# Layer 1 of a two-layer decoder step: the memory queries are projected first, and memory attention of the first half is issued beside the window-query projections

## The chip, the cores and the metric

The kernel runs on one core of one Trainium2 chip. The metric is device time in microseconds (us) of that core. Nothing is shared with other cores. Engines are named as in the profile: PE (TensorE matmul), PEld (TensorE weight load), DVE (VectorE), ACT (ScalarE), POOL (GpSimd), SP (SyncE, which issues nearly all transfers).

## The reference, cut to what matters

Two layers (A: gated linear attention, B: sliding-window attention with sinks) run over 512 prompt tokens and 32 sampled tokens (8 sequences of 4), with model width 1024. Everything is float32. Each layer is a half-weighted SwiGLU block, a mixing block, and a second half-weighted SwiGLU block. The change lies in the mixing block of the second layer (layer 1, B):

```
h = rmsnorm(x, mix_norm[1])
qs, mq = split(h @ b_w_in, [768])          # 12 window heads, 4 memory heads, 64 wide
qs = rope_partial(qs)                      # rotary on 16 of 64 lanes
tok = swa(qs, k_shared, v_shared, sinks)   # window of 128, causal, with a sink per head
mo  = softmax(mq @ mem_k.T / 8) @ mem_v    # 256 memory rows per sequence
x = x + concat([tok, mo]) @ b_w_out
x = x + swiglu_half(x, ffn2)
```

For the prompt the memory keys and values are computed from `mem_prompt`; for the samples they come from `cache_mem_k` and `cache_mem_v`, one set per sequence.

## The kernel before, in words

Tokens are split into two halves: half 0 holds 256 prompt tokens and the 32 sampled ones (288 columns), half 1 the other 256 prompt tokens. Activations lie with the model dimension on the partitions. A weight block (128 x 1024) is loaded by SP, cut by `halved` into a high and a low part (ACT at L298, DVE at L299), and `dense` (L356) multiplies it in three passes per block of 128 rows. One **unit** is one such block: 24 matmuls for one half.

The two halves are run against each other, so that attention of one half goes beside dense work of the other. In `layer`, for layer 1:

- half 1 still has a chunk of its first SwiGLU block to do, the generator `late`: 16 gate and up units and 8 down units (d0 to d7). Seven of them are issued, then half 0's norm, then half 0's whole projection `project(0, ...)` (`in_b`): six window-query units bq0 to bq5, each followed by the rotary step on DVE (`rope`), then two memory-query units bmq0 and bmq1.
- `attend(0, ...)` (`attend_b`) is woven by `weave` with 18 units of `fill`. `fill` is the rest of `late` (17 units), then half 1's norm `enter(1, ...)` and half 1's projection. Two more units (`pad`) follow, so that three units of half 1's projection come before half 0's output projection `out_proj`; the last five come after it.
- `out_proj` for half 0 needs all of half 0's attention.
- The same is then done with half 1's attention against the first chunk of half 0's second SwiGLU block.

`attend_b` itself weaves two streams. One is `swa_prompt`: six groups, three for each 128-token block. A group is scores (L1134), mask and softmax on DVE and ACT (L1155 to L1170), transposes (L1172), masked copies (L1176) and the product with the values (L1142). It uses banks 3 to 5 of the matmul memory, so one group follows another. The other stream is the chain `mem_prompt` (two blocks of scores L649, softmax L654 to L662, transposes L668, values L679), then, in half 0 only, `swa_sample` (L1188 to L1257), then `mem_sample`. `mem_sample` builds masked queries `qb` (L697), multiplies them with the eight cached key tiles `mkc` (loads L703, matmuls L705), does one softmax and two transposes (L720), and multiplies with eight cached value tiles `mvc` (L726, L733). The memory stream uses banks 6 and 7.

The order of instructions on each engine is fixed when the program is built, by a list scheduler that simulates the program. `high_priority(offset=...)` moves work ahead in it: weight cutting and the emptying of dense results by 6000 (`AHEAD`), the norm steps by 6500 (`SOON`), attention issued through `weave` by 3000 (`LEAD`).

Scratch tiles are 97 numbered slots. `self.u` takes the slot at the front of one queue, `drop` puts slots back at its end, and a `Ring` takes several and gives them back when it is closed. Which slot a tile gets depends only on the order in which the code takes and gives back; the first write to a slot waits for the last reader of what lay in it before. The sum of squares for a norm (`stats`) takes a new slot for its first and its eighth tile (L376) and adds the six between into the first (L381). `rstd` sums the two over the partitions with matmuls against ones (L404), goes on with L410 to L430 on DVE and ACT, spreads the result with L416, and `normed` applies it (L438).

Of the kernel before, what the change touches and what calls it, by code (L numbers as in the profile page):

```python
# [163 lines left out]
def chain(*gens):  # L164
    for g in gens:
        yield from g


def take(gen, n):
    for _ in range(n):  # L170
        if next(gen, StopIteration) is StopIteration:
            return
        yield


def drain(*gens):
    for g in gens:
        for _ in g:
            pass
# [42 lines left out]
def chain_weave(*streams):  # L222
    live = [[g, n, 0] for g, n in streams]
    while live:
        s = min(live, key=lambda e: (e[2] + 1) / e[1])
        s[2] += 1
        if next(s[0], StopIteration) is StopIteration:
            live.remove(s)
        else:
            yield  # L230


class Build:
    NU, NV, NLD, NML = 97, 13, 8, 3
    WB = (3, 4, 4, 2)
    MIX = 10
    FIRST, AHEAD, SOON, LEAD = 20000, 6000, 6500, 3000
    FILL = ((6, 1, 7, 2, 6), (7, 2, 5, 0, 9))
    HOMES = ((13, 8, 3), (8, 8, 3))
# [854 lines left out]
    def in_b(self, h, xs, s):  # L1094
        d = self.d
        n = NH[h]
        s.q, s.mq = [], []
        self.rope_tables(h)
        for j in range(6):
            ps, = self.dense(d["b_q"][j], [xs], f"bq{j}")  # L1100
            s.q.append(self.u(n))
            self.rope(ps, s.q[j], h)
            yield
        for j in range(2):
            ps, = self.dense(d["b_mq"][j], [xs], f"bmq{j}")
            s.mq.append(self.copy(self.u(n), ps))
            if j == 1:
                self.drop(xs, self.tabs[h])
            yield

# [156 lines left out]
    def layer(self, l, project, attend, w_out, xs):  # L1267

        s = [Share(), Share()]
        f1, f2 = f"ffn1_{l}", f"ffn2_{l}"  # L1270
        mix, out = {}, {}

        def enter(h, norm):
            with self.tc.high_priority(offset=self.SOON):
                r = self.rstd(h)
                out = self.normed(h, norm, r)
            self.drop(r)
            return out

        def enter_pair(norm, xs):  # L1280
            with self.tc.high_priority(offset=self.SOON):
                r = self.rstd(1)
                xs[1], xs["forms"] = self.pair(norm, r, xs[0])
            self.drop(r)

        def both(tag, xs):
            drain(self.ffn_pair(tag, 1, xs), self.ffn_pair(tag, 2, xs, gathered=(0,)))
            self.drop(xs[0], self.extra)

        lead, pad, hold, last, more = self.FILL[l]  # L1290
        both(f1, xs)
        late = self.ffn(f1, 0, (1,), xs, gathered=(1,), tanh=True)
        mix[0] = enter(0, f"mix_{l}")
        drain(take(late, lead))
        drain(project(0, mix[0], s[0]))

        def second():
            yield from late
            self.drop(xs[1])
            mix[1] = enter(1, f"mix_{l}")  # L1300
            yield from project(1, mix[1], s[1])

        fill, units = second(), EARLY - lead + (22 if l == 0 else 8) - hold - pad
        self.weave(attend(0, s[0]), (take(fill, units), units))
        drain(take(fill, pad))
        self.drop(s[0].q if l else [])
        drain(self.out_proj(w_out, s[0].toks + s[0].mo, 0))
        out[0] = enter(0, f"ffn2_{l}")
        drain(fill)
        if l == 0:  # L1310
            drain(self.late_mem())
        early = self.ffn(f2, 0, (0,), out, tanh=True)
        more += last
        self.weave(attend(1, s[1]), (take(early, EARLY - more), EARLY - more))
        drain(take(early, last))
        self.drop(s[1].q if l else [])
        drain(self.out_proj(w_out, s[1].toks + s[1].mo, 1))
        enter_pair(f"ffn2_{l}", out)
        drain(early)
        both(f2, out)  # L1320

        def final():
            yield from self.ffn(f2, 0, (1,), out, gathered=(1,), tanh=True)
            self.drop(out[1])
        return final()
# [14 lines left out]
    def attend_a(self, h, s):  # L1340
# [2 lines left out]
        return chain_weave((self.attn_a(h, s), 70 if h == 0 else 54), (chain(self.mem_prompt(0, s.mq, s.mo), *extra), 6 + 9 * (h == 0))), \  # L1343
            (76 if h == 0 else 60)

    def attend_b(self, h, s):
        s.mo = self.parts(2, h)
        s.toks = self.parts(6, h)
        extra = [self.swa_sample(s.q, s.toks), self.mem_sample(1, s.mq, s.mo)] if h == 0 else []
        return chain_weave((self.swa_prompt(h, s.q, s.toks), 13),  # L1350
                           (chain(self.mem_prompt(1, s.mq, s.mo), *extra), 6 + 17 * (h == 0))), (37 if h == 0 else 20)

    def run(self):
        nc, d = self.nc, self.d
# [67 lines left out]
        xk = self.normed(1, "kv", r)  # L1422
        drain(take(first, self.MIX))
        drain(self.shared_kv(1, xk))
# [81 lines left out]
```

## Time and profile before

| what | value |
|---|---|
| median of 3 runs | 2154.74 us (2149.47 to 2155.02) |
| profiled execution, own time | 2148.32 us |
| span in the profile | 2146.5 us |
| PE busy, DVE busy, ACT busy | 96%, 72%, 50% of the span |
| mean granted TensorE clock | 0.983 |

The span runs from the first to the last instruction; 1.8 us of the execution's own time lie around it. In the profile L356 is line 356 of the program, `bank<-u,bq0h` is an instruction that writes a bank of the matmul memory from a scratch slot and the high part of weight block bq0, and text in square brackets is idle time of the engine just before the instruction, with what ended it.

### The profile page before, as it was taken

The numbers are of one execution on the slowest core, as the hardware profiler recorded it, in microseconds if no ns is written. First come the engines' busy times: TensorE is split into PE (matmuls) and PEld (weight loads), VectorE is DVE, ScalarE is ACT, GpSimd is POOL, SyncE is SP. The second block draws the span as 40 slices with busy tenths as digits, with TensorE's granted clock in tenths as the row PEclk, the third lists the DMA queues.
The fourth block names the chain that finished last, engine by engine and source line by source line (L and its number), as shares of the span: only waits on it lengthen the run. The fifth ranks groups of instructions, "written<-read, shape, count | busy, mean of one in ns | idle before, by whom it ended". The sixth has DMA issues, their size and how long they took to land.

```text
span 2146.5 us, 41032 instructions
## 1 busy us (share of the span) xinstructions
PE 2065.4 (96%) x16428; PEld 2000.7 (93%) x16428; DVE 1539.5 (72%) x3234; ACT 1067.2 (50%) x2089; POOL 35.8 (2%) x69
## 2 busy tenths in 40 slices
PE   6999999999999998999999999999998999999998
PEld 6999999998799998999999999999986988999998
DVE  7876675576668869757587776665877877966655
ACT  5554444754646645535355553444544544544434
POOL 5000000000000000000000000000000000000000
PEclk9999999999999999999999999999998999999999
DMA  7533253434454342323354523243443434232344
GB/s 230 157 115 109 79 156 118 138 120 148 152 160 159 125 143 79 108 87 103 113 178 142 177 89 114 74 148 122 151 147 105 143 109 128 89 109 79 110 149 128
DMA packets 90496, 273.03 MB, mean 127 GB/s; under 512 B 11408, under 2 KB 25248, under 8 KB 90272
## 3 DMA queue, kind: packets, MB, share of 16 engines
q1 hardware_dynamic: 89728, 269.87, 39.8%
q8 instruction: 129, 2.11, 0.4%
q14 instruction: 63, 0.52, 0.1%
q10 hardware_dynamic: 576, 0.52, 0.1%
HBM read 264.04 MB, written 7.70 MB: 127 GB/s over the span
## 4 chain that ended last, share of the span: by engine, by line
PE 85%; DVE 8%; DMA 4%; ACT 2%; issue 2%; SPq 0%; DVEq 0%; ACTq 0%
PE bank L356 55%; PE bank L342 21%; PE bank L904 1%; PE bank L1142 1%; DVE u L299 1%; PE bank L1134 1%; DMA u19r<-gu_ffn 0%; PE bank L649 0%; DMA u21r<-gu_ffn 0%; DMA u20r<-gu_ffn 0%; PE bank L705 0%; PE bank L416 0%; PE bank L679 0%; PE bank L1030 0%; PE bank L668 0%
## 5 line engine op out<-in xcount | busy, mean ns | idle before, releaser
L298 ACT ACTIVATE u<-u 128x272 fp32r<-128x272 f32 (+3 forms) x328 | 134.0, 422 | 132.5 <-DVE u L537 55.2
L545 DVE SCALAR_TENSOR_TENSOR x<-bank,x 128x16 f32<-128x16 f32 (+2 forms) x192 | 59.7, 342 | 115.0 <-PE bank L356 114.2
L299 DVE TENSOR_TENSOR u<-u,u 128x272 fp32r<-128x272 f32 (+3 forms) x328 | 137.2, 429 | 3.0 <-ACT u L298 1.2
L356 PE MATMUL bank<-u,d0h 128*128 128x272 f32 (+2 forms) x352 | 71.3, 289 | 0.0
L356 PE MATMUL bank<-u,d1h 128*128 128x272 f32 (+2 forms) x352 | 70.3, 288 | 0.0
L356 PE MATMUL bank<-u,d2h 128*128 128x272 f32 (+2 forms) x352 | 68.6, 289 | 0.4 <-DVE x L755 0.4
L356 PE MATMUL bank<-u,d3h 128*128 128x272 f32 (+2 forms) x352 | 68.0, 290 | 0.0
L356 PE MATMUL bank<-u,d4h 128*128 128x272 f32 (+2 forms) x352 | 67.5, 289 | 0.0
L356 PE MATMUL bank<-u,d5h 128*128 128x272 f32 (+2 forms) x352 | 67.3, 289 | 0.0
L356 PE MATMUL bank<-u,d6h 128*128 128x272 f32 (+2 forms) x352 | 67.1, 288 | 0.0
L356 PE MATMUL bank<-u,d7h 128*128 128x272 f32 (+2 forms) x352 | 67.0, 288 | 0.0
L534 ACT ACTIVATE u<-u 128x272 f32<-128x272 f32 x56 | 24.1, 430 | 73.2 <-DVE u L533 73.2
L356 PEld LDWEIGHTS bank<-u,d0h 128*128 128x128 f32 x352 | 56.3, 188 | 0.2
L356 PEld LDWEIGHTS bank<-u,d2h 128*128 128x128 f32 x352 | 55.4, 188 | 0.9 <-issue 0.5
L356 PEld LDWEIGHTS bank<-u,d1h 128*128 128x128 f32 x352 | 56.1, 188 | 0.0
L356 PEld LDWEIGHTS bank<-u,d3h 128*128 128x128 f32 x352 | 55.3, 188 | 0.3 <-DVE x L580 0.3
L356 PEld LDWEIGHTS bank<-u,d4h 128*128 128x128 f32 x352 | 55.4, 188 | 0.0
L356 PEld LDWEIGHTS bank<-u,d5h 128*128 128x128 f32 x352 | 55.2, 188 | 0.1
L356 PEld LDWEIGHTS bank<-u,d6h 128*128 128x128 f32 x352 | 55.2, 188 | 0.0
L356 PEld LDWEIGHTS bank<-u,d7h 128*128 128x128 f32 x352 | 55.1, 188 | 0.1
L356 PE MATMUL bank<-u,d2l 128*128 128x272 f32 (+2 forms) x176 | 51.0, 290 | 0.0
L356 PE MATMUL bank<-u,d4l 128*128 128x272 f32 (+2 forms) x176 | 50.9, 289 | 0.0
(1178 smaller groups left out, 7664.7 us busy)
## 6 DMA issues: line engine op xcount, KB each, us to landing
g0r<-gu_ffn SPq DMA_DIRECT2D x8, 512.0 KB, 3.5
u0r<-gu_ffn SPq DMA_DIRECT2D x8, 512.0 KB, 3.4
g1r<-gu_ffn SPq DMA_DIRECT2D x8, 512.0 KB, 3.4
u1r<-gu_ffn SPq DMA_DIRECT2D x8, 512.0 KB, 3.5
g2r<-gu_ffn SPq DMA_DIRECT2D x8, 512.0 KB, 3.4
u2r<-gu_ffn SPq DMA_DIRECT2D x8, 512.0 KB, 3.9
g3r<-gu_ffn SPq DMA_DIRECT2D x8, 512.0 KB, 3.5
u3r<-gu_ffn SPq DMA_DIRECT2D x8, 512.0 KB, 3.6
```

What stands on the lines that cost most here:

```text
L298: nc.scalar.activation(h, src, AF.Copy)
L299: nc.vector.tensor_tensor(out=l, in0=src, in1=h.bitcast(F32), op=ALU.subtract)
L342: self.nc.tensor.matmul(ps, a[:, k, :], x, start=start and k == 0 and j == 0, stop=k == len(xs) - 1 and j == 2, skip_group_check=True)
L356: self.nc.tensor.matmul(ps, w[:, k, :], x, start=i == 0 and j == 0, stop=i == kc - 1 and j == 2)
L534: nc.scalar.activation(c2, c2, AF.Silu)
L545: nc.vector.scalar_tensor_tensor(out=x, in0=p, scalar=0.5, in1=x, op0=ALU.mult, op1=ALU.add)
L904: nc.tensor.matmul(pv[:, c * half:(c + 1) * half], lhs[:, c * P:(c + 1) * P], second(rhs[:, c * P:(c + 1) * P]), start=True, stop=True)
L1134: nc.tensor.matmul(ps[:, e, P * (1 - back):][:, :P], q[j][64 * half:64 * half + 64, cols], self.keys(kv, half, n - back), start=True, stop ...
L1142: nc.tensor.matmul(dst, self.vt[n - i][:, 64 * kv:64 * kv + 64], pt[i].rearrange("p g t -> p (g t)"), start=i == 0, stop=i == last)
```

## The change

In `in_b` the two memory-query units come first and the six window-query units after them; the rotary tables are loaded after the memory queries, and the normalised input and the tables are given back after bq5. This holds for both halves. For half 0 of layer 1, once bmq0 and bmq1 are issued, a new function `mem_b` builds the chain `mem_prompt` then `mem_sample`, and its first 9 steps (all 6 of `mem_prompt` and the first 3 of `mem_sample`, which end with the matmuls L705) are woven with the six window-query units. `attend_b` for half 0 goes on with the rest of that chain, 6 steps, and then `swa_sample`, 9 steps, woven with `swa_prompt`; it counts 28 steps where it counted 37, against the same 18 units of `fill`. Half 1 keeps its attention as it was.

```diff
@@ class Build
-    MIX = 10
+    MIX, MEM = 10, 9
@@ in_b
         s.q, s.mq = [], []
+        for j in range(2):
+            ps, = self.dense(d["b_mq"][j], [xs], f"bmq{j}")
+            s.mq.append(self.copy(self.u(n), ps))
+            yield
         self.rope_tables(h)
         for j in range(6):
             ps, = self.dense(d["b_q"][j], [xs], f"bq{j}")
             s.q.append(self.u(n))
             self.rope(ps, s.q[j], h)
-            yield
-        for j in range(2):
-            ps, = self.dense(d["b_mq"][j], [xs], f"bmq{j}")
-            s.mq.append(self.copy(self.u(n), ps))
-            if j == 1:
+            if j == 5:
                 self.drop(xs, self.tabs[h])
             yield
@@ layer
-        drain(project(0, mix[0], s[0]))
+        first = project(0, mix[0], s[0])
+        if l == 1:
+            drain(take(first, 2))
+            self.weave(self.mem_b(s[0]), (first, 6))
+        drain(first)
@@ new, and attend_b
+    def mem_b(self, s):
+        s.mo = self.parts(2, 0)
+        s.mem = chain(self.mem_prompt(1, s.mq, s.mo), self.mem_sample(1, s.mq, s.mo))
+        return take(s.mem, self.MEM), self.MEM
+
     def attend_b(self, h, s):
+        s.toks = self.parts(6, h)
+        if h == 0:
+            return chain_weave((self.swa_prompt(h, s.q, s.toks), 13),
+                               (chain(s.mem, self.swa_sample(s.q, s.toks)), 24 - self.MEM)), 37 - self.MEM
         s.mo = self.parts(2, h)
-        s.toks = self.parts(6, h)
-        extra = [self.swa_sample(s.q, s.toks), self.mem_sample(1, s.mq, s.mo)] if h == 0 else []
-        return chain_weave((self.swa_prompt(h, s.q, s.toks), 13),
-                           (chain(self.mem_prompt(1, s.mq, s.mo), *extra), 6 + 17 * (h == 0))), (37 if h == 0 else 20)
+        return chain_weave((self.swa_prompt(h, s.q, s.toks), 13), (self.mem_prompt(1, s.mq, s.mo), 6)), 20
```

## Rows read from the trace of the kernel before

**Rows 1.** The page: busy time of the engines, and the clock in 40 slices.

```profile
PE 2065.4 (96%) x16428; PEld 2000.7 (93%) x16428; DVE 1539.5 (72%) x3234; ACT 1067.2 (50%) x2089; POOL 35.8 (2%) x69
...
PEclk9999999999999999999999999999998999999999
```

**Rows 2.** Windows: stretch, length, busy time by engine, granted clock, DMA share, GB/s.

```profile
1497.80:1526.90 29.10, 29.10 (x226) 28.82 (x225) 22.18 (x46) 11.34 (x18) 0.16 (x1) 1.00 0.45 147
1526.90:1596.00 69.10, 69.10 (x592) 64.01 (x590) 57.85 (x172) 40.08 (x115) 1.42 (x6) 1.00 0.50 155
1596.00:1637.50 41.50, 30.44 (x315) 20.10 (x314) 22.87 (x98) 12.12 (x50) 0.00 (x0) 0.71 0.33 100
...
1757.00:1776.00 19.00, 15.07 (x113) 11.79 (x114) 13.25 (x59) 5.69 (x27) 0.00 (x0) 0.91 0.09 28
```

**Rows 3.** Waits of PE from 1596 to 1638 us: total, times, longest.

```profile
PE bank L1172 <- DVE u L1170: 5.4, 4, 2.4
```

**Rows 4.** Timeline of PE from 1590 us to half 0's output projection.

```profile
1595.83 0.29 PE L356 MATMUL bank<-u,d7l 128*128 128x256 f32 x1
...
1609.21 1.98 PE L705 MATMUL bank<-mkc,u 128*64 128x256 f32 x8 [1.17 <-DMA mkc<-mk]
1610.97 1.92 PE L1142 MATMUL bank<-u,vt 128*64 128x256 f32 x8
...
1613.93 0.83 PE L404 MATMUL bank<-ones,u 128*128 128x1 f32 x6
...
1621.74 1.98 PE L1142 MATMUL bank<-u,vt 128*64 128x256 f32 x8
...
1627.98 0.43 PE L733 MATMUL bank<-mvc,u 128*32 128x64 f32 x16 [2.37 <-DVE we L1160]
...
1635.83 1.77 PE L1142 MATMUL bank<-u,vt 128*64 128x256 f32 x8
...
1637.58 0.36 PE L356 MATMUL bank<-u,bq0h 128*128 128x256 f32 x1
...
1646.82 0.53 PE L356 MATMUL bank<-u,op0h 128*128 128x288 f32 x2 [0.38 <-DVE u L1047]
```

**Rows 5.** Timelines of ACT and DVE in the same stretch.

```profile
1610.42 0.42 ACT L376 ACTIVATE u<-x 128x256 f32<-128x256 f32 x1 [6.24 <-PE bank L705]
...
1596.16 0.42 DVE L580 SCALAR_TENSOR_TENSOR x<-bank,x 128x256 f32<-128x256 f32 x1 [0.26 <-PE bank L356]
...
1630.13 0.15 DVE L410 TENSOR_SCALAR r<-bank 128x2 f32<-128x2 f32 x1
```

**Rows 6.** Tile bmq1h: duration min/median/max in ns, first and last start.

```profile
L356 PE MATMUL bank<-u,bmq1h x32: 274/290/364, 1523.7 to 1687.9; 128*128 128x288 f32 x16, 128*128 128x256 f32 x16
```

**Rows 7.** Single lines, 1497 to 1640 us (L1142: 1545 to 1600).

```profile
L679 PE MATMUL bank<-u,u x32: 272/273/324, 1544.1 to 1563.8; 128*64 128x128 f32 x32
...
L705 PE MATMUL bank<-mkc,u x32: 379/631/689, 1604.6 to 1616.2; 128*64 128x256 f32 x32
...
L1142 PE MATMUL bank<-u,vt x12: 379/404/430, 1549.9 to 1592.8; 128*64 128x256 f32 x12
...
L1203 PE MATMUL bank<-sck,u x48: 270/272/373, 1564.0 to 1581.4; 64*128 64x128 f32 x32, 128*128 128x128 f32 x16
...
L1257 PE MATMUL bank<-stc,scv x32: 202/254/275, 1599.2 to 1602.6; 128*64 128x8 f32 x32
```

**Rows 8.** Groups by line, DVE, 1526.9 to 1596: busy us, mean ns, idle before.

```profile
L654 DVE TENSOR_REDUCE mx<-bank 128x2 f32<-128x512 f32 x4 | 2.7, 686 | 0.7 <-PE bank L649 0.7
...
L662 DVE TENSOR_SCALAR u<-u,sm 128x256 f32<-128x256 f32 x8 | 2.4, 347 | 0.0
...
L697 DVE TENSOR_TENSOR u<-c_bm,u 64x128 f32<-64x128 f32 x8 | 2.3, 284 | 0.1
```

**Rows 9.** Half 1: first scores (timeline), and line L1142 from 1640 to 1780 us.

```profile
1656.26 1.16 PE L1134 MATMUL bank<-u,u 64*128 64x128 f32 x16
...
L1142 PE MATMUL bank<-u,vt x48: 379/379/657, 1692.8 to 1775.0; 128*64 128x256 f32 x48
```

## The prediction

> **What bounds the kernel now.** Read the page first: PE is busy 96% of the span and granted full clock nearly throughout, with one dent in the clock line about three quarters of the way [rows 1]. A change that removes no work can gain only where PE waits or runs at the lower of its two levels, so the next view is the windows around the changed code [rows 2]. In the first two stretches, half 0's projection and the rest of `late`, PE is busy for every microsecond at full clock. Then 41.5 us follow in which PE is busy for 30.44 at a mean granted clock of 0.71 (2.4 GHz is 1.00, 1.2 GHz is 0.50). That is the tail of half 0's attention, and the only big hole near the change. Three units of half 1's projection come behind it (1637.58 to 1646.82, 9.3 us [rows 4]), and only then half 0's output projection.
>
> Why is the tail bare? The timeline of PE has the last matmul of `late` at 1595.83 and the first of half 1's projection at 1637.58 [rows 4]. Between them PE waits most for softmax steps, 5.4 of its 11.1 idle us [rows 2, 3], with no dense unit to put there, since half 1's projection needs its norm. The timelines of ACT and DVE show why the norm is late [rows 5]: the last update of x is at 1596.16, but its square (L376) stands until 1610.42 behind L705. The count of slots explains that: the eighth square takes the first slot given back by `qb`, and L705 reads `qb`. Then the sums (L404) come at 1613.93 [rows 4], and their reader L410 stands in DVE's order behind attention until 1630.13 [rows 5]. From L410 to the first projection matmul it is 7.5 us. Without the two delays the norm would need from 1596.6 about 0.4 (square), 0.8 (sums) and 7.5 us, so some 10 instead of 42.
>
> **The change, part by part.**
>
> *Memory queries first, both halves.* The same eight units, in another order: bmq0 and bmq1 end about 20 us earlier than before, where the last began at 1523.7 [rows 6] and the projection ended at 1526.9, 3.2 us on. They end at about 1507: from 1497.8 two units of 3.2 and one unit of `late`, 3.1 by the pace of half 1's three units [rows 4]. Each window query comes 6.4 us later. Cost on PE: nothing.
>
> *`mem_prompt` beside the projection.* Its last matmuls started at 1563.8 [rows 7], and all lay inside the stretch where PE is full [rows 2]; they are moved from one full stretch to another, so nothing is won on PE. DVE takes L654, L662 and L697 with it, 7.4 us [rows 8], plus some 1.3 of small steps, into a stretch where it had 29.10 - 22.18 = 6.9 us free [rows 2]. The cutting of weights goes ahead of it, so I cost this at nothing; what hides it is that weights are cut some units ahead. If that cover is gone, PE waits for the overflow, 8.7 - 6.9 = 1.8 us. The bounds are 0 and 2.
>
> *The first three steps of `mem_sample`.* Eight key loads (256 KB each), L697 and the 32 matmuls L705 leave the tail. In the tail L705 took 1.98 us for 8 [rows 4]; at full clock a 256-column matmul in a dense unit takes 0.128 us (9.24 for 72), so 32 cost 4.1 us in the full stretch. Behind them the chain goes on with the value matmuls L733, eight tiles at 0.43 us [rows 4], 3.5 us. `late` then ends up to 7.6 us later than 1596; I take 6, so 1602. The loads join the weight loads in SP's order and wait for three buffers; behind them stand weight loads, and behind those the cutting and the units. The DMA share there is 0.45 to 0.50 against 0.33 in the tail [rows 2]; I cost them at nothing, and 1.2 us (the one wait on such a load [rows 4]) if three weight buffers ahead don't cover.
>
> *Slots.* Counting takes and returns through the new order: the window attention's two rings, 11 slots, now get two slots of a rotary step, the four of `qb`, the two memory queries, two of the last rotary step and one of the normalised input. So the first group of `swa_prompt` can't write its weights before the last L705. By the durations of before, `mem_prompt` takes 1563.8 - 1526.9 = 37 us and L705 12 [rows 7]: 1507 + 37 + 12 = 1556, and about 4 for the rest of the group puts its first value product at 1560. Before it was at 1549.9 [rows 7]. The window chain thus starts about 10 us later. On the other side, the eighth square now gets the slot of `mem_sample`'s probabilities, whose last reader, the transposes L720, is then long past. The 14 us of waiting on L705 go.
>
> *The tail.* The first three value products were about 21 us apart (1549.9 to 1592.5, twelve matmuls in three groups [rows 7]), those in the tail 10.8 apart at best (1610.97 to 1621.74 [rows 4]); the step between 1592.5 and 1610.97 had L705 in front, 6 us with its wait. With the first at 1560 the third falls at 1602, the fourth at 1613, the sixth at 1634.5, and the output projection can start at about 1636. Attention hence ends about where it did (1637.5): what the memory work gives back at the end, the later start takes. The gain is that half 1's norm starts at 1602 and its three units, 9.3 us, run from about 1612 inside the tail and no longer behind it. 1646.8 - 1636.2 = 10.6 us. `swa_sample` comes last now; it took 39 us beside dense work (1564.0 to 1603 [rows 7]) and can start about 20 us after L705 (the rest of `mem_sample` lay between the last L705 at 1616.2 and 1637.5 [rows 4, 7]), at 1576, so it ends by 1615 and does not set the end. Bounds: 1.3 if the three units stay behind, 21 if the window chain is one group ahead.
>
> *A rule beside these rows.* The Trainium skill, page "Perfetto Trace Analysis", section "Identifying the Most-Contended Engine", says that matmul busy time flatters PE and that weight-load busy time should be read. In the tail that is 20.10 of 41.5 us against 30.44 [rows 2]: a hole of 21.4 us by the rule and 11.1 by the row. In the full stretches both are near full, so the rule changes only how much the tail can give.
>
> *Half 1.* Its first window scores started at 1656.26, during half 0's output projection [rows 9]. They need bq0 and bq1; bq1 now comes after that projection. `mem_prompt` can go first in its place. I cost this at nothing, with bounds of 6 us lost (the first group of scores some 20 us later, of which most was waiting: its first value product came only at 1692.8 [rows 9]) and 4 gained (PE idle 3.9 us in the last stretch [rows 2]).
>
> Sum: 2148.3 (the profiled execution) - 10.6 = 2137.7. The median of the runs shown is 6.4 above the profiled execution, so about 2144 as a median.
>
> **The rivals.**
>
> *No change (0.26).* Half 1's norm stays behind attention: L410 stood 15 us in DVE's order after its sums were there [rows 4, 5], with DVE half idle, and a new fixed order can repeat that. The three units then stay behind the tail: gain 1.3, 2153. The Trainium skill, page "TensorE: Matmul & The Clock Gate", the specification table at its head, gives VectorE a strictly ordered queue; by that rule such an instruction can't be overtaken, and the trace agrees with the 15 us.
>
> *More (0.12).* With the memory stream lighter, the window chain is a group ahead when `late` ends. One step of 10.8 us leaves the tail: gain 21, 2133. That uses the whole hole that weight loads show [rows 2]. Against it: the slots make that chain start late.
>
> *Slower (0.18).* The slot wait costs more than I take. The first group waits for L705, and six groups follow in one row. Each us by which its value product comes after 1560 moves the end by one. From 1571 on there is no gain; at 1580, two dense steps late, it is 9 us slower, 2164. For it: `mem_prompt` competes on DVE with six rotary steps, 22.18 of 29.10 us busy already [rows 2]. Against it: without window groups in its way it may run faster than 37 us.
>
> **How the numbers follow.** The forecast has 0.44, the three rivals 0.26, 0.12 and 0.18. The time is that of the forecast, 2144. Its own range is 2136 to 2151. The range for all reaches from 2128 (more than 21 us gained, with half 1's 4) to 2161, which leaves out most of the slower case. A change of 0.3%, 6.5 us, is about what a measurement of this kernel can tell from none: faster (below 2148.3) takes the forecast and the better rival, 0.56; slower (above 2161) 0.17; 0.27 lies between.
>
> **What would show it.** Right: L376 for the eighth square no longer waits on L705; units bmq0, bmq1 and bq0 of half 1 lie among the last window groups, not behind them; the stretch from the end of `late` to half 0's output projection falls from 51 us to about 34, at a granted clock above 0.71; the first L1142 near 1560. Wrong: L410 again far behind L404; PE waits for cut weights between 1498 and 1535; the first L1142 after 1571; half 1's attention ending later against its output projection. Most likely to fail is the date of the first window group, since I took it from durations in another surrounding.

## The result and the profile after

The changed kernel takes 2159.92 us (median of 9 runs, 2155.94 to 2162.02), the kernel before in the same runs 2154.09 (9 runs). The ratio is 1.0031, 95% interval 1.0019 to 1.0042: 5.8 us slower by the medians, where 2144 and a gain was forecast.

One caution ahead of the rows. The two profiled executions differ before the first changed instruction: L410 of half 0's own norm stands at 1477.82 us in the one and at 1483.02 in the other, with the same order of instructions on PE up to there. So what follows is measured from the first matmul of half 0's projection, 1497.8 in the kernel before and 1501.5 in the changed one. From there to the last L510 (the matmuls with which the next SwiGLU block takes over two banks of half 1's attention) it is 277.5 and 285.5 us: 4.3 of the 8 us are lost up to half 0's output projection (149.0 against 153.3), 3.7 behind it (128.5 against 132.2).

The page after the change, to be read against [rows 1]:

```profile
PE 2074.4 (96%) x16428; PEld 2005.3 (93%) x16428; DVE 1541.2 (71%) x3234; ACT 1064.4 (49%) x2089; POOL 34.7 (2%) x69
...
PEclk9999999999999999999999999999997999999999
```

The same number of instructions, but PE is busy 9 us longer. That fits more time at the lower level of the clock: the mean granted clock is 0.980 for 0.983, and the dent has gone from 8 to 7. The windows show the stretches: the projection with the rest of `late`, the tail, and half 1's three units. Columns as in [rows 2].

```profile
1501.40:1605.20 103.80, 103.55 (x949) 95.20 (x949) 82.56 (x221) 52.20 (x134) 0.20 (x1) 1.00 0.57 180
1605.20:1643.90 38.70, 26.84 (x182) 19.20 (x181) 24.82 (x105) 13.88 (x58) 0.10 (x1) 0.65 0.07 22
1643.90:1654.80 10.90, 10.55 (x74) 10.34 (x73) 5.16 (x16) 4.22 (x11) 0.00 (x0) 0.82 0.01 2
```

The full stretch is longer by the memory work that moved into it, as forecast, and PE is idle for only 0.25 us of it. But the tail behind it has lost those matmuls (182 for 315 in [rows 2]) and hardly shrunk, and the three units stand behind it as before, partly at the lower clock (10.9 us at 0.82). The timeline of PE over the tail:

```profile
1605.22 0.36 PE L404 MATMUL bank<-ones,u 128*128 128x1 f32 x2
...
1605.83 0.83 PE L404 MATMUL bank<-ones,u 128*128 128x1 f32 x6
1607.51 0.65 PE L1142 MATMUL bank<-u,vt 128*64 128x256 f32 x4 [0.84 <-DVE u L1176]
...
1612.92 0.43 PE L1172 MATMUL bank<-c_ident,u 128*128 128x128 f32 x2 [3.67 <-DVE u L1170]
...
1615.74 1.98 PE L1142 MATMUL bank<-u,vt 128*64 128x256 f32 x8 [0.52 <-DVE u L1176]
...
1623.87 1.45 PE L1172 MATMUL bank<-c_ident,u 128*128 128x128 f32 x4 [4.14 <-DVE u L1170]
1625.84 1.97 PE L1142 MATMUL bank<-u,vt 128*64 128x256 f32 x8 [0.52 <-DVE u L1176]
...
1642.04 1.95 PE L1142 MATMUL bank<-u,vt 128*64 128x256 f32 x7
...
1654.80 0.53 PE L356 MATMUL bank<-u,op0h 128*128 128x288 f32 x2 [0.35 <-ACT u L362]
```

The value products of four of the six window groups lie behind the end of `late`, where it was three; PE waits for their softmax. Why so late, and why didn't half 1's norm fill the hole? ACT and DVE:

```profile
1605.38 0.40 ACT L376 ACTIVATE u<-x 128x256 f32<-128x256 f32 x1
...
1525.45 0.76 DVE L1155 COPY_PREDICATED bank<-masks,neg 128x256 f32<-128x256 uint8 x2
...
1563.95 0.42 DVE L712 TENSOR_REDUCE smx<-bank 128x1 f32<-128x256 f32 x1
...
1564.68 0.41 DVE L1158 TENSOR_REDUCE wx<-bank 128x2 f32<-128x256 f32 x1
...
1605.43 0.56 DVE L1215 SCALAR_TENSOR_TENSOR u<-bank,u 128x160 f32<-128x160 f32 x2 [0.47 <-PE bank L1208]
...
1622.78 0.75 DVE L1216 TENSOR_REDUCE vx<-u 128x1 f32<-128x160 f32 x3
...
1633.23 0.14 DVE L410 TENSOR_SCALAR r<-bank 128x2 f32<-128x2 f32 x1
```

Four things are to be seen. The eighth square (L376) no longer waits for L705: that step of the forecast holds. The first window group is masked at 1525.45 (L1155), and its maximum (L1158), which needs nothing else, comes 39 us later, directly behind mem_sample's maximum L712. In `swa_sample` the last masked scores are ready at 1605.99 (L1215), and their maxima (L1216) come 16.8 us later, behind the maxima of the fifth window group; its last value product then starts at 1641.9, in the tail, where the forecast had it done by 1615. And the norm's L410 comes 27.4 us after the start of its last sums (16.2 before, [rows 4, 5]). In the kernel before the same pattern was there to be seen and was overlooked: L1155 of the first group at 1513.40, its L1158 at 1534.58, directly behind the two maxima of `mem_prompt`.

```profile
1513.40 0.77 DVE L1155 COPY_PREDICATED bank<-masks,neg 128x256 f32<-128x256 uint8 x2 [0.33 <-PE bank L1134]
...
1533.25 0.69 DVE L654 TENSOR_REDUCE mx<-bank 128x2 f32<-128x512 f32 x1
...
1534.58 0.40 DVE L1158 TENSOR_REDUCE wx<-bank 128x2 f32<-128x256 f32 x1
```

What these steps have in common is where they write: L410, L654, L712, L1158 and L1216 (in `swa_sample`) each open a tile of `self.small` (L281), one ring of 24 buffers under one tag for all streams. The theory tested below is that a ring hands out its buffers in the order in which the code issues their first writes. In the changed kernel `mem_b` issues all tiles of `mem_prompt` ahead of the first window tile, the step behind it issues the one of L712, also ahead, and the norm's tiles come behind those of window groups issued before them. The rivals are the scratch slots, which the prediction counted, DVE's load, and half 1's new order of projections. One more, that 24 buffers are simply too few, is tested by no run, since every edit of the rings also adds buffers; counting the code speaks against it. Between half 0's own norm and the first window maximum only 13 tiles are taken (three by that norm, eight by `mem_prompt`, two by `mem_sample`), so the ring can hardly have run out there.

### The profile page after: what moved, and what is told of

Same layout as the page of the kernel before. It is cut to its first block, busy times and chain, and to the rows that moved or that the text cites. A ratio compares the mean times of both kernels' runs of the same rounds, so it can differ in the third digit from the quotient of the medians.

```text
span 2158.5 us, 41028 instructions
## 1 busy us (share of the span) xinstructions
PE 2074.4 (96%) x16428; PEld 2005.3 (93%) x16428; DVE 1541.2 (71%) x3234; ACT 1064.4 (49%) x2089; POOL 34.7 (2%) x69
## 4 chain that ended last, share of the span: by engine, by line
PE 49%; DVE 7%; DMA 3%; issue 1%; ACT 1%; DVEq 0%; ACTq 0%; SPq 0%
PE bank L356 32%; PE bank L342 13%; PE bank L1142 1%; DMA u20r<-gu_ffn 1%; DMA u18r<-gu_ffn 1%; DMA u19r<-gu_ffn 1%; DMA u21r<-gu_ffn 1%; PE bank L1134 1%; DVE u L299 0%; PE bank L416 0%; PE bank L1172 0%; DVE u L537 0%; PE bank L1203 0%; DVE u L535 0%; PE bank L404 0%
## 5 line engine op out<-in xcount | busy, mean ns | idle before, releaser
L298 ACT ACTIVATE u<-u 128x272 fp32r<-128x272 f32 (+3 forms) x328 | 133.9, 421 | 139.9 <-DVE u L537 61.4
```

The source lines that it names most:

```text
L298: nc.scalar.activation(h, src, AF.Copy)
```

## The experiments

All times are ratios to the kernel before on the same chip, with a 95% interval; from the profile of each run come distances in us. **Group 1** is the first value product L1142, **late** the last d7 matmul and **op** the first matmul of half 0's output projection (in norm_ring the first behind the stall), all from the projection's first matmul; **norm** is from the start of the last row of sums L404 to L410; **half 1** is from op to the last L510; **sum** is op and half 1 together.

| kernel | ratio | group 1 | late | norm | op | half 1 | sum |
|---|---|---|---|---|---|---|---|
| before | 1 | 52.1 | 98.0 | 16.2 | 149.0 | 128.5 | 277.5 |
| the change | 1.0031 (1.0019 to 1.0042) | 76.8 | 102.8 | 27.4 | 153.3 | 132.2 | 285.5 |
| h0_new | 0.9968 (0.9954 to 0.9981) | 45.4 | 113.8 | 11.4 | 145.2 | 128.9 | 274.1 |
| before_h1_new | 1.0018 (1.0007 to 1.0029) | 52.1 | 98.0 | 16.2 | 149.7 | 131.0 | 280.7 |
| order_only | 0.9979 (0.9966 to 0.9993) | 45.4 | 112.5 | 12.5 | 145.2 | 132.8 | 278.1 |
| h1_old | 1.0032 (1.0020 to 1.0043) | 76.8 | 103.8 | 27.4 | 153.4 | 127.6 | 281.0 |
| mem6 | 1.0013 (1.0003 to 1.0022) | 61.4 | 105.2 | 19.9 | 147.8 | 130.7 | 278.5 |
| norm_ring | 1.0033 (1.0020 to 1.0047) | 76.5 | 105.7 | 1.5 | 150.2 | 133.5 | 283.7 |
| window_ring | 1.0033 (1.0020 to 1.0047) | 62.7 | 108.6 | 0.9 | 147.4 | 137.9 | 285.3 |
| two_rings | 1.0031 (1.0017 to 1.0046) | 63.0 | 108.7 | 0.9 | 146.9 | 133.5 | 280.4 |
| mem_rings | 1.0075 (1.0062 to 1.0088) | 70.3 | 106.6 | 24.4 | 153.9 | 136.2 | 290.1 |
| window_prompt_rings | 0.9970 (0.9958 to 0.9982) | 63.9 | 109.6 | 1.4 | 140.4 | 134.6 | 275.0 |
| all_rings | 0.9974 (0.9963 to 0.9985) | 63.1 | 108.4 | 1.4 | 137.8 | 134.3 | 272.2 |
| h1_old_all | 0.9947 (0.9928 to 0.9965) | 63.1 | 108.9 | 1.4 | 141.5 | 124.9 | 266.4 |
| before_norm_ring | 0.9987 (0.9975 to 0.9998) | 51.9 | 97.8 | 0.9 | 141.3 | 133.0 | 274.3 |
| before_all_rings | 0.9927 (0.9915 to 0.9939) | 35.2 | 116.5 | 0.9 | 138.9 | 124.9 | 263.8 |
| before_rings_h1_new | 0.9969 (0.9958 to 0.9981) | 35.2 | 113.6 | 0.9 | 136.3 | 131.9 | 268.3 |
| before_rings_h0_new | 0.9945 (0.9928 to 0.9963) | 45.3 | 120.3 | 2.4 | 142.5 | 122.6 | 265.2 |

Sum and ratio agree to 4 us or better but for order_only (0.6 us longer by its one profile, 4.5 shorter by the ratio); where they differ the ratio, made of many runs, decides. The column op is not the end of half 0's attention in every kernel: in norm_ring, window_ring, two_rings, window_prompt_rings, all_rings, h1_old_all and before_norm_ring the output projection starts ahead of the last group's value product. In these and in before_all_rings it takes 28.9 to 30.9 us from op to the projection's last matmul, in the other ten 26.8 to 27.4; so there 2 to 4 us of what op gains come back in the column half 1.

Since the order of instructions is fixed when the program is built, each edit shifts the whole order, not only the step that it names.

### The rings, on the changed kernel

**norm_ring.** Only the norm's tiles leave the shared ring.

```diff
@@ rstd, L405
-        v, s, t = (self.small("r", 3)[:, :len(blocks)] for _ in range(3))
+        v, s, t = (w[:, :len(blocks)] for w in (lambda w: [w[:, 3 * i:3 * i + 3] for i in range(3)])(self.up.tile([P, 9], F32, tag="smn", name="r", bufs=1)))
```

> The changed kernel, in which only the three small tiles of the normalisation (L405) leave the shared ring of 24 small tiles and have a ring of their own. Theory: the norm's first small step (L410) stands 27 us behind its sums because the shared ring hands its buffers out in the order in which the code issues them, and the last window group's tiles were issued ahead of it. Then L410 follows the sums within about 3 us, half 1's first three units (9.3 us) run ahead of the last two groups of half 0's window attention, and the time falls by about 8 us against the changed kernel, to about 2152 (0.997 to 1.000 of the kernel before). Rival: DVE's load, or the order in which the planner wants the steps, holds L410; then it stays 15 us or more behind the sums and the time stays at 2160 (1.003). Second rival: the units come early but the six window groups are pushed back by as much; then half 1's projection starts at about 1612 and the output projection still at about 1654, and the time is 2158 to 2160.

The mechanism came as expected, the gain did not. L410 follows its sums by 1.5 us and the three units run in the tail, from 1619.42. PE's timeline:

```profile
1612.94 0.83 PE L404 MATMUL bank<-ones,u 128*128 128x1 f32 x6
...
1619.42 0.39 PE L356 MATMUL bank<-u,bmq0h 128*128 128x256 f32 x1 [2.43 <-ACT u L298]
...
1638.49 1.45 PE L1172 MATMUL bank<-c_ident,u 128*128 128x128 f32 x4 [4.96 <-DVE u L1170]
1640.46 1.98 PE L1142 MATMUL bank<-u,vt 128*64 128x256 f32 x8 [0.52 <-DVE u L1176]
...
1655.83 0.85 PE L356 MATMUL bank<-u,op0h 128*128 128x288 f32 x2
```

And two windows, with the units and behind them:

```profile
1612.30:1632.60 20.30, 16.97 (x137) 14.99 (x137) 15.83 (x53) 12.02 (x30) 0.10 (x1) 0.92 0.09 30
1632.60:1660.40 27.80, 21.36 (x135) 15.83 (x134) 17.11 (x70) 9.47 (x41) 0.00 (x0) 0.65 0.21 67
```

Then PE has nothing dense left (it issues six matmuls of op0 and stops) and the last window groups run bare, 27.8 us at a granted clock of 0.65. The hole has moved, not shrunk: the second rival of the expectation.

**window_ring.** Only the window groups' tiles leave, one tile for each pair's maximum, sum and sink; the shared ring shrinks to 18 for room.

```diff
@@ swa_probs, L1156
-        mx, sm, es = self.small("wx", 2), self.small("ws", 2), self.small("we", 2)
+        mx, sm, es = (lambda w: [w[:, 2 * i:2 * i + 2] for i in range(3)])(self.up.tile([P, 6], F32, tag="smw", name="wx", bufs=12))
```

> The changed kernel, in which the three small tiles of each window group (L1156) have a ring of their own (and the shared ring has 18 buffers in place of 24, for room). Theory of the shared ring: the first group's maximum (L1158) waited 39 us behind its mask step (L1155) because its tile comes after those of mem_prompt and mem_sample in the ring. Then L1158 follows L1155 within about 3 us, and the first value product (L1142) comes as soon as L705 has given the slots back, at about 1564 in place of 1578: one group less in the tail, 8 to 12 us under the changed kernel, 2148 to 2152 (0.997 to 0.999). Rival, the scratch slots alone (the step that the prediction named): L1158 is early, but the first L1142 stays at 1575 or later, and the time at 2158 to 2161. Second rival: the planner's order sets it; L1158 stays behind L712.

DVE, ACT and PE:

```profile
1525.49 0.76 DVE L1155 COPY_PREDICATED bank<-masks,neg 128x256 f32<-128x256 uint8 x2
1526.29 0.76 DVE L1158 TENSOR_REDUCE wx<-bank 128x2 f32<-128x256 f32 x2
...
1554.87 0.37 ACT L1164 ACTIVATE u<-bank,wx 128x128 f32<-128x128 f32 x1 [0.48 <-PE bank L705]
...
1564.14 0.65 PE L1142 MATMUL bank<-u,vt 128*64 128x256 f32 x2
```

The maximum now follows the mask by 0.8 us in place of 39, and nothing but the rings was changed. The exponential behind it (L1164) then waits for PE's L705, the reader of the slot that it writes. That is the wait for slots that the prediction counted; it is real, and it stood hidden behind the ring's. The first pair of group 1 comes at 62.7, forecast were 62.2 (1560 less 1497.8); its second pair follows at 71.0. L410, too, follows its sums at once (0.9), and so does `swa_sample`'s L1216: they had waited for the window's tiles. Still the time stays: op comes 5.9 us earlier than in the changed kernel, and half 1 gives 5.7 back (3.9 and 3.7, if measured to the end of half 0's output projection).

**two_rings.** Both edits together (shared ring 17).

> The changed kernel with own rings for the normalisation and the window attention alone; the memory attention's tiles stay in the shared ring (17 buffers). norm_ring and window_ring each gave nothing, all_rings 12 us against the changed kernel. Theory: two waits stand one behind the other in half 0 (the first window group's and the norm's), and either alone keeps the end; with both gone the output projection starts about 138 to 141 us after the projection's first matmul (changed kernel 153.4, all_rings 137.8), and the time is 0.996 to 0.998 of the kernel before. Rival: the memory streams' own rings made the difference; then it stays at 1.000 to 1.003.

The theory that these two waits are all was wrong: 1.0031. Both are gone (63.0 and 0.9), and op still comes only at 146.9.

**all_rings.** Besides, own rings for `mem_prompt` (L653), `mem_sample` (L711) and `swa_sample` (L1211), in the same form; 14 buffers stay shared.

> The changed kernel, in which each stream has a ring of small tiles of its own: the normalisation, the window attention, the memory attention over the prompt, that over the samples, and the sample rows' window attention (the shared ring has 14 buffers for the rest). Theory of the shared ring: both delays go, the norm's 27 us and the first window group's 39 us; half 1's three units run before the last two groups, and the output projection starts 10 to 15 us earlier than in the changed kernel. Half 1's own loss of about 3.6 us stays. 2145 to 2150 (0.996 to 0.998 of the kernel before). Rival: the tail is bound by the window chain itself, whatever the rings; 2156 to 2160.

As expected: 12 us under the changed kernel, op at 137.8. The sixth group's value product comes only at 144.0, beside the output projection.

**window_prompt_rings.** Which of them does it? Own rings for the window groups and `mem_prompt` alone (16 shared); the norm stays in the shared ring.

```diff
@@ mem_prompt, L653
-                mx, sm = self.small("mx", 2), self.small("sm", 2)
+                mx, sm = (lambda w: [w[:, 2 * i:2 * i + 2] for i in range(2)])(self.up.tile([P, 4], F32, tag="smm", name="mx", bufs=4))
```

> The changed kernel with own rings for the window attention and for mem_prompt only; the norm stays in the shared ring (16 buffers). Theory: the coupling that counts is between those two streams (each one's maxima wait for the other's tiles); the norm waited only because the window's tiles stood ahead of it. Then it runs like all_rings: output projection about 138 us after the projection's first matmul, 0.996 to 0.998 of the kernel before. Rival: the norm or the sample rows need their own ring too; 1.000 to 1.003.

These two are enough: 0.9970. The norm, still in the shared ring, follows its sums by 1.4 us, so here, as in window_ring, it had waited for the window's tiles. The windows, against those of the changed kernel above (full stretch, tail with the three units in it, half 1):

```profile
1501.10:1610.70 109.60, 107.74 (x975) 97.67 (x973) 88.13 (x252) 54.97 (x146) 0.28 (x3) 1.00 0.52 166
1610.70:1641.40 30.70, 29.52 (x216) 24.91 (x216) 21.86 (x85) 17.15 (x55) 0.00 (x0) 0.72 0.14 45
1641.40:1777.00 135.60, 127.46 (x995) 116.69 (x994) 105.33 (x302) 65.47 (x167) 0.00 (x0) 0.97 0.37 121
```

The tail is 30.7 us with 1.2 idle; in the changed kernel tail and units took 49.6 (38.7 and 10.9). The last window group is no longer in it: its value product comes 6.1 us behind op.

**mem_rings.** The other way round: `mem_prompt` and `mem_sample` leave (20 shared), window groups and norm stay together.

> The changed kernel with own rings for the memory attention alone (mem_prompt and mem_sample); window attention and norm share the ring (20 buffers). Theory: the first window group no longer waits for the memory maxima, but its two pairs and the norm stay coupled to the ring, and L410 stays behind the last window groups: the three units stay behind the tail, and about half of all_rings' 12 us come, 0.998 to 1.001. Rival: the memory tiles alone were the trouble; 0.996 to 0.998. Second rival: nothing comes; 1.002 to 1.004.

All three guesses missed: 1.0075, the slowest of all. DVE and ACT:

```profile
1528.99 0.42 DVE L1158 TENSOR_REDUCE wx<-bank 128x2 f32<-128x256 f32 x1
...
1564.08 0.42 DVE L1158 TENSOR_REDUCE wx<-bank 128x2 f32<-128x256 f32 x1
...
1564.37 0.37 ACT L1164 ACTIVATE u<-bank,wx 128x128 f32<-128x128 f32 x1 [1.52 <-PE bank L705]
```

The first pair of group 1 is early, its second pair 35 us later, together with the first pair's exponential. The first write of the first pair's sum (`ws`, filled by L1164, which waits for L705's slot) is issued between the two maxima. That fits the theory: a ring that hands out in order holds a stream up behind its own tiles, too, and here passes the slot wait on. It also shows whose order it is: the first pair's `we`, made after `ws` but written ahead of it in the code (L1160), is written at 1530.80, before the stall. Too few buffers can't be the cause here, since from half 0's norm on only six of the ring's 20 have been taken (three by that norm, three by the first pair). In the rings of their own the three are one tile, so this can't happen there; how much of window_ring's effect is that and how much the separation was not tried apart. The norm stays 24.4 us behind. Yet this delay isn't where the time goes: group 1 and op come at 70.3 and 153.9 for 76.8 and 153.3 in the changed kernel, and of the 9.5 us between the two ratios the profiles show 4.6, of which 4.0 lie in half 1. Why half 1 is longer is open.

### The parts of the change

**h0_new.** Of the change only half 0's order of projections; memory attention and half 1 as before.

```diff
@@ in_b
+        def mqs():
...
+        def qs():
...
+        yield from chain(*((qs(), mqs()) if h else (mqs(), qs())))
```

> The kernel before (shared ring) with, of the change, only half 0's new order of projections: memory queries first, the memory attention where it was. order_only (both halves) gave 0.998 and before_h1_new 1.002; if the parts add up, half 0's order alone gives 0.995 to 0.997, because mem_prompt can start without waiting for the six window queries while the window groups keep their early start; the 1.003 of the whole change then comes from moving the memory attention ahead (1.005 by itself). Rival: the parts don't add; 0.998 to 1.000.

0.9968: this part alone is a gain of 7 us. `mem_prompt` starts 20 us earlier by the profile (first L649 13.2 us after the projection's first matmul in place of 33.5), so do its maxima, and with them the first window group (45.4 in place of 52.1).

**before_h1_new.** Only half 1's order (the same edit with the halves exchanged).

> The kernel before (shared ring) with, of the change, only half 1's new order of projections. h1_old got nothing back by the old order, before_rings_h1_new lost 9 us by the new one with rings of their own. Theory: the shared ring hides this cost, since half 1's window groups wait for other tiles of the ring anyway: 0.999 to 1.001. Rival: the new order costs half 1 in this kernel too, the 3.7 us that the two profiles show; 1.001 to 1.003.

The rival: 1.0018. Half 1's stretch is 131.0 for 128.5.

**order_only.** Both halves' order, no memory work moved.

> The kernel before with the new order of projections in both halves and nothing else of the change: mem_prompt and mem_sample stay where they were. Theory: half 1 loses its 3.7 us; in half 0 each window query comes 6.4 us later and nothing is won, so the window chain starts up to 6 us later: 3 to 9 us slower, 1.002 to 1.004. Rival (the prediction's costing): the order alone costs nothing; 0.999 to 1.001.

0.9979, faster, which neither case had: the two parts before it add up to 0.9986. So moving the memory attention is what costs: from order_only to the change 0.0052, from h0_new to h1_old 0.0064, 11 to 14 us.

**h1_old.** The changed kernel, half 1 in the old order.

> The changed kernel with half 1's projection back in its old order (six window queries, then the two memory queries); half 0 stays as changed. Theory: the new order costs half 1 by itself, because its six window groups run one behind the other and their first scores now wait for bq0 and bq1 behind the output projection; from the output projection's first matmul to the last L510 it was 132.2 us in the changed kernel and 128.5 in the kernel before. Then this stretch is about 128.5 again and the time 3 to 4 us under the changed kernel, about 2156 on the scale of 2154 before (1.000 to 1.002). Rival: half 1 is late only since half 0's attention ends later; then the stretch stays at 132 and the ratio at 1.003.

By the ratio nothing comes back (1.0032), by the profile 4.6 us of half 1's stretch do (127.6 for 132.2). The interval of the difference, about 0.0016 either way or 3.4 us, nearly reaches from the one to the other; this kernel alone doesn't decide it.

**mem6.** The changed kernel with `mem_sample`'s first three steps left where they were.

```diff
-    MIX, MEM = 10, 9
+    MIX, MEM = 10, 6
```

> The changed kernel with MEM at 6 in place of 9: mem_prompt is still woven beside the projection, but the first three steps of mem_sample (key loads, L705, its maximum L712) stay in the attention behind it, so no tile of mem_sample is issued ahead of the first window group. Shared ring: the first L1158 then waits for mem_prompt's second maximum only, so it comes about 56 to 62 us after the half's own norm in place of 81.7, the first value product at about 75 to 80 in place of 95, and one group leaves the tail: 6 to 10 us under the changed kernel, 0.998 to 1.0005. Rival: the first group gains nothing since the second still stands behind mem_sample's steps; 1.002 to 1.004.

Between the cases: 1.0013, 3.9 us under the changed kernel. Group 1 comes at 61.4 in place of 76.8, and op 5.5 us earlier. (L712 belongs to `mem_sample`'s fourth step, not its third; with 6 it, too, is issued behind the first window group.)

### The rings without the change, and half 1's order

**before_norm_ring.** norm_ring's edit on the kernel before.

> The kernel before with an own ring for the normalisation alone. Theory: where the window groups are early (first value product 72 us after the norm, 95 in the changed kernel), the norm's wait is the one that counts; L410 then follows the sums and half 1's three units run ahead of the last groups: 4 to 9 us faster, 0.996 to 0.998. Rival, as in norm_ring: the last groups are pushed back by as much; 0.999 to 1.001.

Between the cases, 0.9987. The units run early, and the last two value products are pushed back, from 123.9 and 138.0 to 127.6 and 148.0. The output projection begins 7.7 us earlier but ahead of the last group, and its end comes only 3.7 us earlier; that is why half 1, counted from op, looks 4.5 us longer.

**before_all_rings.** All five rings on the kernel before.

> The kernel before with the same five rings. Theory of the shared ring: the same coupling held there too (its first window group's L1158 came 21 us after L1155, right behind the maximum of mem_prompt, and L410 came 15 us behind the sums), so it gains as well, and the part of the change that the rings don't take away is what all_rings then shows against this kernel. 2144 to 2150 (0.995 to 0.998). If the ring matters only with the new order, it stays at 2152 to 2156 (0.999 to 1.001). Against all_rings: if the loss of half 1 is the change's own, this kernel is about 3 to 4 us faster than all_rings.

0.9927, 2135.82 us against 2151.34: better than expected, the fastest of all, and with nothing of the change in it. The windows (full stretch, tail, half 1):

```profile
1500.70:1617.20 116.50, 116.50 (x969) 107.01 (x968) 94.48 (x292) 58.05 (x172) 1.46 (x5) 0.96 0.43 135
1617.20:1639.60 22.40, 18.25 (x234) 15.92 (x233) 16.04 (x48) 12.07 (x27) 0.10 (x1) 0.85 0.46 152
1639.60:1764.50 124.90, 121.60 (x979) 112.96 (x978) 101.71 (x292) 64.33 (x168) 0.00 (x0) 1.00 0.40 131
```

The window chain starts at 35.2, the tail is 22.4 us, and op comes at 138.9, as early as in all_rings (137.8).

**before_rings_h1_new.** The same with half 1's new order.

> The kernel before with a ring of small tiles for each stream, and of the change only half 1's new order of projections. Theory: half 1's order is what costs all_rings its 9 us against before_all_rings; then from the output projection's first matmul to the last L510 it is about 134 us in place of 124.9, and the ratio to the kernel before 0.996 to 0.998 (before_all_rings: 0.993). Rival: half 1's order alone costs nothing, as the prediction had it; 0.992 to 0.994.

0.9969 for 0.9927: 9 us lost, as the theory had it; half 1 131.9 for 124.9.

**h1_old_all.** all_rings with half 1 in the old order.

> The changed kernel with both corrections: a ring of small tiles for each stream, and half 1's projection in its old order. Theory: half 0 reaches the output projection 157.8 us after its own norm as in all_rings (the kernel before 169.0), and half 1 takes 125 us from there as in before_all_rings (124.9) and not the 134.3 of all_rings: 9 us under all_rings, 0.992 to 0.994 of the kernel before, the same as before_all_rings within 2 us. The change in half 0 then is worth about 1 us (157.8 against 158.9). Rival: the 9 us between all_rings and before_all_rings come from half 0 (its chains end in another order), and it stays at 0.996 to 0.998.

Half 1's stretch is 124.9 as expected; of the 9 us the ratio shows 5.8 (0.9947 for 0.9974). It doesn't reach before_all_rings, so half 0's changes are worth nothing once the rings are apart. Whether they lose 0.002 is not clear, since the two intervals overlap.

**before_rings_h0_new.** before_all_rings with half 0's new order.

> The kernel before with a ring of small tiles for each stream and, of the change, only half 0's new order. If order and rings add up: 0.988 to 0.991, faster than before_all_rings (0.993). Rival: with rings of their own the streams no longer care about the order; 0.992 to 0.994.

0.9945: the order that gave 7 us in the shared ring gives nothing here; that it is 0.0018 above before_all_rings is within the two intervals. That gain, too, was one of the shared ring.

## Why the prediction was wrong

**What held.** `late` ended 4.8 us later (6 taken). The eighth square is free of L705. The moved loads and the cutting of weights cost next to nothing (PE idle 0.25 us in 103.80). The wait for slots is as counted: with the ring out of the way the first pair of group 1 comes at 62.7 to 63.9 us, forecast 62.2. The sum for half 0 is met in number but not along its path. The output projection was forecast at 138.4 (1636.2 less 1497.8) and all_rings has it at 137.8. But there it starts ahead of the sixth group, whose value product comes at 144.0 and not at 136.7; up to the end of the output projection all_rings is 9.0 us ahead of the kernel before, for the 10.6 of the sum. That the one number agrees so well is partly luck.

**The step that failed** is the part *Slots*, and with it the gain that *The tail* builds on it: it held that the scratch slots decide when the first window group and the norm can start. It counted one kind of buffer, the slots, and not the ring of small tiles that all streams share. That ring held group 1 behind `mem_sample`'s maximum (76.8 us for 62.2), `swa_sample` behind window groups, and half 1's norm behind the last of them, so the tail kept its length and the three units stayed behind it. Two rivals named two of these effects: *Slower* says that the first group comes after 1571 (it came at 1578.25, or 1574.6 by the distance from the projection), and *No change* that the norm stays behind attention, L410 late again.

The larger price is that of the second. The first three groups came 14.4 and 14.8 us apart, not 21, so the chain made up for its late start: the third and fourth value products stand at 106.0 and 114.3 us, forecast 104.2 and 115.2, and the sixth at 140.4 for 136.7. The output projection missed its forecast by 14.9 us (153.3 for 138.4); 3.7 of them lie in the window chain, and 11.2 behind it, where the three units now run. By the rule of *Slower*, each us past 1560 off the forecast gain of 10.6, the 14.6 us would have cost 4.0, and half 0 lost 4.3; with the chain caught up, this agreement is a coincidence. Nor would the norm alone have saved it: in norm_ring the units run early, and the sixth value product moves back by 12.5 us.

*No change* gave DVE's fixed order as the reason; the order was the symptom. The Trainium skill, page "TensorE: Matmul & The Clock Gate", the specification table at its head, says that VectorE's queue is strictly ordered; the traces agree, since L410 stands 27.4 us behind its sums while DVE is busy for only 24.82 of the 38.7 us of the tail. But norm_ring and window_ring show that where it stands in that order is set by the ring.

**The second step that failed** is *Half 1*, costed at nothing with 6 us lost as a bound. The new order puts half 1's first value product 61.0 to 65.2 us behind op in the eleven kernels that have it; with the old order it is 36.6 to 46.1 in the other seven. Most of that is absorbed, as assumed, but not all: five pairs of kernels that differ in this alone show half 1's stretch 2.5, 3.9, 4.6, 7.0 and 9.4 us longer (before_h1_new, order_only, the change, before_rings_h1_new and all_rings against their partners), and the ratios 0.0018, 0.0011, -0.0001, 0.0042 and 0.0027. So by the ratios 0 to 4 us in the shared ring, and 6 to 9 once nothing else holds the window chain.

**How the loss adds up.** Along one path of the runs (h0_new, order_only, the change) half 0's order gives -0.0032, half 1's 0.0011 and moving the memory attention 0.0052; along the other (h0_new, h1_old, the change) -0.0032, 0.0064 for the move and -0.0001 for half 1's order. Both must end at the measured 0.0031, so their sums prove nothing; what they show is that the move is the loss by either.

**What stays open.** Why two_rings gains nothing where window_prompt_rings, with `mem_prompt` in place of the norm, gains 13 us. Shown is that `mem_prompt`'s tiles must leave, and that with two_rings both waits are gone. A wait of `mem_prompt`'s maxima is hardly the reason: its last pair comes at 36.4 us in two_rings and at 33.9 in window_prompt_rings, well before the first value products (63.0 and 63.9). The groups behind lie further apart, 15.3 us from the second group's maxima to its value product in place of 11.2, and what pushes them apart is not known.

## What to carry to other kernels

A list of what a moved step needs is complete only with every pool that it takes a buffer from: a small shared ring orders streams that have no data in common, and an instruction that stands on an idle engine with its inputs long ready points to it. Look for that pattern in the profile before moving work, and take the coupling away first; here that alone gave 15.5 us, and the move none on top of it. Where a stall is lifted from a chain, ask what the next lock is: norm_ring and window_ring each lifted theirs cleanly, and the time didn't move.

## What was not expected

A wait can be handed on within one stream (mem_rings: the second maximum 35 us behind the first, at no data of its own), and a mended half of a coupling can be worse than none (1.0075). Filling the holes does not by itself bring the clock back: the granted clock is 0.65 in the tail of the changed kernel (PE busy 26.84 us of 38.7) and in the bare stretch of norm_ring (21.36 of 27.8), but also only 0.72 in the filled tail of window_prompt_rings (29.52 of 30.7), against 1.00 in the changed kernel's full stretch (103.55 of 103.80), 1.00 standing for 2.4 GHz and 0.50 for 1.2.
